# The second layer's MLP as seven block products: float32 block sums on GpSimd, split into halves before each product

## The chip, the cores and the metric

One Trainium2 chip, of which one core is used. The metric is the device time of one execution in microseconds; lower is better. Engines are named as in the profile: PE (TensorE, matmuls), PEld (its weight loads), DVE (VectorE), ACT (ScalarE), POOL (GpSimd), SP (SyncE, which here only issues DMAs).

## The reference

A backbone of two layers over 1024 latent tokens and 256 context tokens, width 1024, all in float32. Layer 0 mixes with two kinds of attention, layer 1 with a state-space scan and a gated unit (GLU); each layer ends in an MLP with a hidden width of 4096:

```python
def _mlp(h, w1, w2):
    return jnp.square(jax.nn.relu(h @ w1)) @ w2
...
        h2 = _rmsnorm(x, norm2_g[i], NORM_EPS) * (1.0 + sc2) + sh2
        x = x + g2 * _mlp(h2, mlp_w1[i], mlp_w2[i])
...
    return _rmsnorm(x, final_g, NORM_EPS)
```

In layer 1 only the 1024 latent tokens go on, so its MLP is two matrix products, 1024 x 1024 by 1024 x 4096 and back.

## The kernel before

The residual stream `xl` stays on chip, feature by token; `xv1(ct, b)` (line 1083) is feature tile `ct` (128 of 1024) of the half `b` (512 tokens). Float32 operands are multiplied as three products of halves: a value is rounded to the matmul's own 32-bit format (`hi`, on ACT) and the rest is subtracted out (`lo`, on DVE), and `mm3` (line 312) issues hi·hi, hi·lo and lo·hi for each pair of tiles, each a 128x128 weight against 128x512 tokens.

`mlp` (line 1124) runs over 16 slices `f` of the hidden width, 256 columns each. For each it loads two 512 KB pages of W1 and two of W2 (`weights`, line 301, which also splits them), multiplies the normed input halves `Hh[b]` and `Hl[b]` (eight feature tiles) by W1, takes Relu and Square on ACT, the same square and the remainder on DVE (lines 1140 to 1143), multiplies by W2 and adds each result tile to the stream with one DVE instruction (`add_x`, line 1091), a multiply by the gate and an add, straight from the accumulator. For layer 1 nothing else runs beside it.

Before it stands `glu` (line 1580), which goes through half 0 and then half 1. After each half, `follow` and `rstd_steps` (lines 391 and 322) collect squares, sum them on PE (`n_st`, `n_tk`), take a reciprocal root and spread it (`n_bc`), and `scaled` (line 435) writes the normed input: a DVE multiply, a POOL scale and shift, then the split into `Hh` and `Hl` (`to_H`, line 1093). Half 0's norm runs beside half 1's GLU; half 1's runs while the MLP has only half 0 to work on. After the last slice the same steps serve the final norm (`final`, line 1608), whose results are stored on SP.

The order of instructions is chosen by a scheduler that takes what is ready, by priority, except in stages that use `Plan` (line 112). There each step carries an engine, a fixed cost, a rank (its due time), what it comes after and which buffers it takes and gives; `order` (line 142) lists the steps by the time at which they could start by those costs plus 0.05 of their rank, and every engine's queue is laid down in that order. A queue is worked off strictly in order. Before the change the attention and the scan (`ssm`, line 1408) use it. Memory comes from pools stacked from the left and the right; a tile laid on memory of an earlier pool waits for the last user of what it covers.

## Time and profile before

| | us |
|---|---|
| three runs before | 3135.32, 3137.86, 3138.17 |
| median of them | 3137.86 |
| the profiled execution | 3133.75 |
| its span, first to last instruction | 3132.0 |
| in it: layer 1's MLP, from the GLU's last matmul to its own last | 2402.8 to 3114.1 |
| in it: final norm and stores after that | 3114.1 to 3132.0 |

The mean granted clock of the span is 0.98. All positions in the text are microseconds from the span's start in the profiled execution.

### The profile page before, as it was taken

How to read it: one execution, taken by the hardware profiler on the slowest of the kernel's cores; microseconds unless marked ns; L12 is line 12 of the kernel's file. 1: busy time of each engine (PE TensorE's matmuls, PEld its weight loads, DVE VectorE, ACT ScalarE, POOL GpSimd, SP SyncE). 2: the span in 40 equal slices, each digit the busy share in tenths (PEclk: the TensorE clock that was granted, in tenths of full speed). 3: DMA queues.
4: the chain of work that ended last, by engine and by line, in shares of the span. 5: the costliest groups of instructions: out<-in, count | busy, mean ns of one | idle time of the engine just before them, and what ended most of it. 6: DMA issues, size and time to landing. Idle time of an engine off the chain costs nothing.

```text
span 3132.0 us, 46329 instructions
## 1 busy us (share of the span) xinstructions
PE 2949.1 (94%) x17736; PEld 2435.7 (78%) x17736; DVE 1844.6 (59%) x3225; ACT 969.1 (31%) x1843; POOL 1128.4 (36%) x2314
## 2 busy tenths in 40 slices
PE   7999998889999999999999999777899999999998
PEld 4878887777778778777888888566787888888886
DVE  4887677997653655455454454699524554455444
ACT  3322125766652311111211211445323212212122
POOL 3352224555432577777884000477323000000001
PEclk9999999999999999999999999888999999999999
DMA  6356564324533234334111101566212111111111
GB/s 237 108 199 228 199 216 132 88 71 118 158 94 123 88 106 122 107 121 92 60 59 54 41 30 37 174 184 179 85 61 88 53 42 54 41 54 53 42 54 54
DMA packets 171149, 321.53 MB, mean 103 GB/s; under 512 B 34560, under 2 KB 97056, under 8 KB 170928
## 3 DMA queue, kind: packets, MB, share of 16 engines
q1 hardware_dynamic: 165840, 302.24, 30.9%
q0 software_dynamic: 5088, 16.34, 1.6%
...
## 4 chain that ended last, share of the span: by engine, by line
PE 77%; DVE 13%; issue 3%; DMA 3%; ACT 2%; POOL 2%; SPq 0%; DVEq 0%; POOLq 0%; ACTq 0%
PE m_acc L317 17%; PE m_acc L318 16%; PE m_acc L319 16%; DVE s_ab L1506 2%; PE at_bank L740 2%; PE at_sc L732 2%; PE g_acc L319 2%; PE g_acc L317 2%; PE g_acc L318 2%; PE ip_acc L317 2%; PE ada_acc L269 2%; PE ip_acc L318 2%; PE ip_acc L319 2%; PE at_bank L1023 2%; DVE s_ab L1494 1%
## 5 line engine op out<-in xcount | busy, mean ns | idle before, releaser
L1091 DVE SCALAR_TENSOR_TENSOR xl<-m_acc,m,xl 128x512 f32<-128x512 f32 x512 | 378.7, 748 | 222.0 <-PE m_acc L319 221.7
L317 PE MATMUL m_acc<-hid_h,w_hi 128*128 128x512 f32 (+1 forms) x1280 | 476.8, 372 | 0.0
L317 PE MATMUL m_acc<-Hh,w_hi 128*128 128x512 f32 (+1 forms) x1280 | 473.4, 370 | 0.9 <-ACT Hh L453 0.9
L318 PE MATMUL m_acc<-hid_l,w_hi 128*128 128x512 f32 (+1 forms) x1280 | 472.4, 369 | 0.0
L318 PE MATMUL m_acc<-Hl,w_hi 128*128 128x512 f32 (+1 forms) x1280 | 471.8, 369 | 0.5 <-DVE Hl L454 0.5
L319 PE MATMUL m_acc<-hid_h,w_lo 128*128 128x512 f32 (+1 forms) x1280 | 471.8, 369 | 0.0
L319 PE MATMUL m_acc<-Hh,w_lo 128*128 128x512 f32 (+1 forms) x1280 | 471.4, 368 | 0.0
L308 ACT ACTIVATE w_hi<-w_raw 128x1024 fp32r<-128x1024 f32 x196 | 202.5, 1053 | 796.1 <-PE m_acc L318 688.8
L309 DVE TENSOR_TENSOR w_lo<-w_raw,w_hi 128x1024 fp32r<-128x1024 f32 x196 | 244.3, 1261 | 214.3 <-ACT w_hi L308 204.9
L1142 DVE TENSOR_TENSOR m_r<-m_r 128x512 f32<-128x512 f32 (+1 forms) x160 | 103.9, 651 | 407.8 <-ACT hid_h L1141 407.6
L425 POOL TENSOR_TENSOR rs_y<-n_v,mhalf 128x4 f32<-128x4 f32 (+1 forms) x13 | 12.4, 950 | 763.3 <-DVE n_v L373 763.3
L317 PEld LDWEIGHTS m_acc<-hid_h,w_hi 128*128 128x128 f32 x1280 | 241.2, 188 | 56.7 <-issue 15.2
L317 PEld LDWEIGHTS m_acc<-Hh,w_hi 128*128 128x128 f32 x1280 | 241.4, 189 | 47.1 <-issue 5.8
L318 PEld LDWEIGHTS m_acc<-hid_l,w_hi 128*128 128x128 f32 x1280 | 241.3, 189 | 44.3 <-issue 5.0
L318 PEld LDWEIGHTS m_acc<-Hl,w_hi 128*128 128x128 f32 x1280 | 241.5, 189 | 40.9 <-DVE Hl L454 2.1
L319 PEld LDWEIGHTS m_acc<-hid_h,w_lo 128*128 128x128 f32 x1280 | 241.3, 189 | 40.4
L319 PEld LDWEIGHTS m_acc<-Hh,w_lo 128*128 128x128 f32 x1280 | 241.4, 189 | 40.0
L1140 ACT ACTIVATE m_r<-m_acc 128x512 f32<-128x512 f32 (+1 forms) x160 | 87.9, 551 | 440.4 <-PE m_acc L319 436.4
L317 PE MATMUL ip_acc<-Hh,w_hi 128*128 128x512 f32 (+1 forms) x384 | 141.6, 370 | 4.1 <-ACT Hh L453 4.1
L318 PE MATMUL ip_acc<-Hl,w_hi 128*128 128x512 f32 (+1 forms) x384 | 138.1, 360 | 1.4 <-DVE Hl L454 1.2
L319 PE MATMUL ip_acc<-Hh,w_lo 128*128 128x512 f32 (+1 forms) x384 | 137.5, 359 | 0.0
L732 PE MATMUL at_sc<-at_k,at_q 128*128 128x256 f32 (+2 forms) x608 | 125.1, 336 | 10.9 <-ACT at_p L822 4.3
...
## 6 DMA issues: line engine op xcount, KB each, us to landing
w_raw<-in_w_dram SPq DMA_DIRECT2D x128, 512.0 KB, 4.1
...
```

What stands on the lines that cost most here:

```text
L269: nc.tensor.matmul(acc[32 * q:32 * q + 32, 256 * half:256 * half + 256], self.act[:, 4 * kg + q, :], r[:, q, :], start=(kg == 0), stop=(kg ...
L308: nc.scalar.activation(hi[:, j], r, AF.Copy)
L309: nc.vector.tensor_tensor(lo[:, j], r, hi[:, j].bitcast(F32), ALU.subtract)
L317: nc.tensor.matmul(out, lh, rh, start=first and i == 0, stop=False)
L318: nc.tensor.matmul(out, lh, rl, start=False, stop=False)
L319: nc.tensor.matmul(out, ll, rh, start=False, stop=last and i == n - 1)
L732: PE.matmul(sc[:, c:c + n], qd["q"][:, m, hl, qo:qo + P], k["k"][m][:, k0:k0 + n], start=(hl == 0), stop=(hl == 1))
L740: PE.transpose(tp[:kw, P * j:P * j + P], p[:, c0 + P * j:c0 + P * j + kw], self.ident)
L1023: PE.matmul(grp["pv"][64 * hh:64 * hh + 64, u, :], hd["v"][:kw, vt, 64 * hh:64 * hh + 64], st["aT", (hh, i)][:kw, P * (j % 4):P * (j % 4) ...
L1091: nc.vector.scalar_tensor_tensor(xv, av, gate, xv, op0=ALU.mult, op1=ALU.add)
L1140: nc.scalar.activation(r[:, :n], acc[:, :n], AF.Relu)
L1142: nc.vector.tensor_tensor(r[:, :n], r[:, :n], r[:, :n], ALU.mult)
```

## The change

Layer 1's MLP is done by Strassen's scheme in Winograd's form. Each of four slices `f` of 1024 hidden columns has two units, one for W1 and one for W2, and a unit is a product of two 1024x1024 matrices cut into 2 x 2 blocks of 512: seven block products in place of eight, with weight sums s1 to s4 and token sums t1 to t4 of 512x512 blocks, and sums of the results. The host lays the weights out as 1 MB blocks (`w1b`, `w2b`); those of layer 0 keep their pages.

A product is four steps (one for each tile of 128 along the inner width); a step is 12 matmuls, three for each of four accumulator banks. Before each step a weight tile and a token tile, 128x512 each, are split by one ACT and one DVE instruction into one of four slots per operand. The sums run on POOL, float32, 32 of 128x512 per unit. In W1 units the token blocks are the normed input in float32 (`Hr`); the token sums go to r1, r2, r3. In W2 units they are the hidden blocks and most sums are made in place. Products that share terms accumulate on the banks of an earlier one after it has been copied out (`ON`). Product 1 of a W2 unit, which goes to three blocks of the stream, is copied out scaled by ACT into the four r2 tiles, and 12 POOL instructions add it to the stream; the other six are added by DVE as before. The order of products is 1, 6, 2, 7, 5, 4, 3, in the first unit 1, 2, 6, 7, 5, 4, 3. All of it is laid out by a `Plan`.

The GLU's `scaled` now writes `Hr` on POOL, without the split. `Hr` (two halves of 16 KB per partition) takes the memory under the GLU's weight pages; the new weight blocks and split slots take that of `Hh` and `Hl`, the other new tiles that of the pages. The final norm's tiles are views of tiles that are then free.

```diff
+    a["w1b"] = g["mlp_w1"][1].reshape(2, 4, P, 4, 2, 512).transpose(3, 4, 0, 2, 1, 5).reshape(4, 2, 2, P, 2048)
+    a["w2b"] = g["mlp_w2"][1].reshape(4, 2, 4, P, 2, 512).transpose(0, 4, 1, 3, 2, 5).reshape(4, 2, 2, P, 2048)
...
+            o = to(ct) if to else t[:, :n]
+            nc.gpsimd.tensor_scalar(o, t[:, :n], G[:, ct, m:m + 1], self.mv(i, part, ct, m), op0=ALU.mult, op1=ALU.add)
+            if put:
+                put(ct, o)
...
+    ON = {2: 1, 7: 6, 4: 7, 3: 5}
+
+    def mlp_s(self, mp, wp, ps):
...
+        for q in "ab":
+            blocks += [wp.tile([P, 4, 512], F32, name=f"st_w{q}{j}") for j in range(2)]
+            slots[q] = [wp.tile([P, 2, 512], F32R, name=f"st_{q}{j}") for j in range(4)]
...
+        r2 = [mp.tile([P, 512], F32, name=f"st_r2{t}") for t in range(4)]
...
+        plan = Plan(rings, lead=10.0)
...
+        for u in range(8):
+            f, second, last = u // 2, u % 2, u == 7
+            order = (1, 2, 6, 7, 5, 4, 3) if u == 0 else (1, 6, 2, 7, 5, 4, 3)
...
+            for (m, k), p in (((0, 0), 1), ((1, 0), 6), ((1, 1), 6), ((0, 1), 2)):
+                ld[m, k] = plan.add("D", 5.6, at[p] - 30, F(load, m, k), take=["A"], issue=0.7)
...
+                    if p == 6:
+                        made["s1", t] = plan.add("G", 1.4, r - 14, lambda t=t, A=A: vt(s1[:, t], A[1, 0][:, t], A[1, 1][:, t], ALU.add),
...
+                    if second:
+                        gh = lambda k, n: [(f"h{k}{n}{t}", hm["take", k, n, t])]
+                        if p == 6:
+                            made["t1", t] = plan.add("G", 1.4, r - 13, F(vt, r1[t], b12, b11, ALU.subtract), [hd(0, 1), hd(0, 0)], take=[f"r1{t}"])
+                            made["t3", t] = plan.add("G", 1.4, r - 12.5, F(vt, b12, b22, b12, ALU.subtract), [hd(1, 1), made["t1", t]])
+                            made["t2", t] = plan.add("G", 1.4, r - 12, F(vt, b11, b22, r1[t], ALU.subtract), [made["t1", t], made["t3", t], *sp[1, t, "b"]])
...
+                    def hi(w, t=t, sl=sl, av=av, bv=bv, A=A, tm=tm):
+                        sl[w] = T(w, slots[w]), av(A, t) if w == "a" else tm["r3", t] if bv is None else bv
+                        S.activation(sl[w][0][:, 0], sl[w][1], AF.Copy)
+
+                    def lo(w, sl=sl):
+                        V.tensor_tensor(sl[w][0][:, 1], sl[w][1], sl[w][0][:, 0].bitcast(F32), ALU.subtract)
...
+                        hs[w] = plan.add("S", 0.56, r - 8, F(hi, w), after, take=[w])
+                        ls[w] = plan.add("V", 0.66, r - 7.5, F(lo, w), [hs[w]], give=give)
...
+                        for mt in range(4):
+                            c = slice(P * mt, P * mt + P)
+                            for i, (x, y) in enumerate(((l[:, 0, c], h[:, 0]), (l[:, 0, c], h[:, 1]), (l[:, 1, c], h[:, 0]))):
+                                PE.matmul(bk[p][mt], x, y, start=(p not in self.ON and t == 0 and i == 0), stop=(t == 3 and i == 2), skip_group_check=True)
...
+                        if p == 3:
+                            x = plan.add("V", 0.72, rk, F(ev, c12, c12, 3), [pe, made["u2", t]], give=giveX(5))
+                            relu2(c12, c12, rk + 0.5, [x], (0, 1, t))
+                    else:
+                        if p == 1:
+                            for m, g in ((0, g1), (1, g2)):
+
+                                o = r2[(2 * t + m) % 4]
+                                c = plan.add("S", 0.58, rk + 0.1 * m, lambda o=o, g=g, ps_=ps_: S.activation(o, ps_(1), AF.Copy, scale=g), [pe], take=[f"r2{(2 * t + m) % 4}"])
+                                outs.append(c)
+                                for x in ((x12,) if m == 0 else (x21, x22)):
+                                    made.setdefault("xu", []).append(plan.add("G", 1.4, rk + 2 + m, F(vt, x, x, o, ALU.add), [c], give=[(f"r2{(2 * t + m) % 4}", c)]))
...
-            self.scaled(lambda ct: self.xv1(ct, b), 512, 1, 1, 0, bc, sp, self.to_H(b))
+            self.scaled(lambda ct: self.xv1(ct, b), 512, 1, 1, 0, bc, sp, to=lambda ct: self.Hr[b][:, ct])
...
+            rp = es.enter_context(net.pool("hr"))
+            net.Hr = [rp.tile([P, KT, 512], F32, name=f"hr{b}") for b in range(2)]
...
-                with net.pool("mlp1") as mp:
-                    net.mlp(1, (0, 1), net.xv1, ps, mp, lambda: None, lambda: net.follow(net.xv1, ps, mp, lambda b, bc: net.final(b, bc, mp)))
+            hs.close()
+            with net.pool("mlp1") as mp, net.pool("mlp1w", side="right") as wp, net.pool("ps5", space=PSUM) as ps:
+                net.mlp_s(mp, wp, ps)
```

## Rows read from the trace of the kernel before

**Rows 1.** The page, part 1: busy time, share of the span and instructions.
```profile
PE 2949.1 (94%) x17736; PEld 2435.7 (78%) x17736; DVE 1844.6 (59%) x3225; ACT 969.1 (31%) x1843; POOL 1128.4 (36%) x2314
```
**Rows 2.** Windows: stretch, us, busy PE PEld DVE ACT POOL, clock, DMA share, GB/s.
```profile
2402.80:2428.10 25.30, 21.50 (x98) 14.91 (x96) 13.67 (x23) 8.79 (x14) 10.85 (x10) 1.00 0.13 42
...
2441.00:3093.00 652.00, 652.00 (x2878) 540.11 (x2877) 322.26 (x418) 131.08 (x182) 0.00 (x0) 1.00 0.15 47
...
3114.10:3132.00 17.90, 5.09 (x25) 3.72 (x24) 6.75 (x13) 1.40 (x3) 1.70 (x2) 0.59 0.43 165
...
2200.00:2222.00 22.00, 13.24 (x65) 11.00 (x63) 16.36 (x26) 7.52 (x14) 10.88 (x13) 0.84 0.08 28
```
**Rows 3.** Groups by line, 2402.8 to 3132: count | busy us, mean ns | idle before.
```profile
L317 PE MATMUL m_acc<-hid_h,w_hi 128*128 128x512 f32 x512 | 199.5, 390 | 0.0
...
L1091 DVE SCALAR_TENSOR_TENSOR xl<-m_acc,m,xl 128x512 f32<-128x512 f32 x256 | 189.2, 748 | 104.7 <-PE m_acc L319 104.7
...
L1143 DVE TENSOR_TENSOR hid_l<-m_r,hid_h 128x512 fp32r<-128x512 f32 x64 | 44.0, 689 | 1.6
L1141 ACT ACTIVATE hid_h<-m_r 128x512 fp32r<-128x512 f32 x64 | 40.1, 629 | 1.5
L1140 ACT ACTIVATE m_r<-m_acc 128x512 f32<-128x512 f32 x64 | 37.8, 593 | 185.9 <-PE m_acc L319 184.4 <-DVE hid_l L1143 1.5
```
**Rows 4.** Windows of the MLP's accumulators alone, the first stretch.
```profile
2402.80:2428.10 25.30, 18.94 (x73) 12.90 (x72) 0.00 (x0) 0.14 (x1) 1.00 0.13 42
```
**Rows 5.** Timeline of DVE, operations in a row: start, us.
```profile
2430.78 1.29 DVE L1143 TENSOR_TENSOR hid_l<-m_r,hid_h 128x512 fp32r<-128x512 f32 x2
...
3123.44 5.36 DVE L1618 SCALAR_TENSOR_TENSOR f_o<-xl,vecs,n_bc 128x512 f32<-128x512 f32 x8 [2.17 <-PE n_bc L382]
```
**Rows 6.** Timeline of POOL in the GLU.
```profile
2239.06 1.29 POOL L1604 TENSOR_TENSOR xl<-xl,g_sg 128x512 f32<-128x512 f32 x1 [24.48 <-DVE g_sg L1602]
2249.16 2.20 POOL L1604 TENSOR_TENSOR xl<-xl,g_sg 128x512 f32<-128x512 f32 x1 [8.81 <-DVE g_sg L1602]
2252.10 1.29 POOL L356 TENSOR_TENSOR n_sq<-n_sq 128x512 f32<-128x512 f32 x1 [0.74 <-ACT n_sq L351]
```
**Rows 7.** Timeline of DVE in the GLU, the operations beside those.
```profile
2239.17 2.26 DVE L309 TENSOR_TENSOR w_lo<-w_raw,w_hi 128x1024 fp32r<-128x1024 f32 x1 [0.19 <-ACT w_hi L308]
...
2249.00 1.22 DVE L309 TENSOR_TENSOR w_lo<-w_raw,w_hi 128x1024 fp32r<-128x1024 f32 x1
```
**Rows 8.** Timeline of POOL in the final norm.
```profile
3106.83 2.55 POOL L1620 TENSOR_TENSOR f_o<-xl,f_r 128x512 f32<-128x512 f32 x2 [2.51 <-ACT f_r L1613]
```
**Rows 9.** Timeline of DVE beside them (`m_acc` is an accumulator).
```profile
3107.55 0.75 DVE L1091 SCALAR_TENSOR_TENSOR xl<-m_acc,m,xl 128x512 f32<-128x512 f32 x1
```
**Rows 10.** The chain that ended last, between GLU and MLP: start, us, what.
```profile
2408.72 1.07 PE n_st L336 x8
...
2410.91 0.80 PE n_tk L371 x8
...
2413.64 1.17 PE n_bc L382 x8
...
2427.42 0.64 ACT Hh L453
```
**Rows 11.** Timeline of POOL: the scalings of half 1.
```profile
2415.63 2.82 POOL L448 TENSOR_SCALAR n_t<-n_t,G,m 128x512 f32<-128x512 f32 x3 [2.63 <-DVE n_t L447]
```
**Rows 12.** Timeline of PE: the scan's last readout, the GLU's first matmul.
```profile
2217.92 0.61 PE L1532 MATMUL s_y<-s_T,s_U 128*128 128x128 f32 x4
...
2221.91 0.50 PE L317 MATMUL g_acc<-Hh,w_hi 128*128 128x512 f32 x1 [1.82 <-ACT w_hi L308]
```
**Rows 13.** Timeline of SP: issues of the GLU's pages.
```profile
2197.42 0.33 SPq L307 DMA_DIRECT2D w_raw<-in_glua_dram  x1
...
2223.14 0.33 SPq L307 DMA_DIRECT2D w_raw<-in_glua_dram  x1
```
**Rows 14.** Timeline of ACT: the first use of such a page.
```profile
2226.85 1.06 ACT L308 ACTIVATE w_hi<-w_raw 128x1024 fp32r<-128x1024 f32 x1 [4.04 <-DMA w_raw<-in_glua_dram]
```

More of the change, by code (lines that the diff above doesn't have):

```diff
@@ L54, in host_layout @@
     a["glub"] = pages(g["glu_w_b"][0])
-    a["w1"] = np.stack([pages(g["mlp_w1"][i]) for i in range(2)])
-    a["w2"] = g["mlp_w2"].reshape(2, 32, P, D)
+    a["w1"] = pages(g["mlp_w1"][0])
+    a["w2"] = g["mlp_w2"][0].reshape(32, P, D)
+    a["w1b"] = g["mlp_w1"][1].reshape(2, 4, P, 4, 2, 512).transpose(3, 4, 0, 2, 1, 5).reshape(4, 2, 2, P, 2048)
+    a["w2b"] = g["mlp_w2"][1].reshape(4, 2, 4, P, 2, 512).transpose(0, 4, 1, 3, 2, 5).reshape(4, 2, 2, P, 2048)
     rpb = g["na_rpb"][0]
@@ L196, in run, with __init__, tile @@
                 s["fn"]()
+class Views:
+    def __init__(self, pool, **views):
+        self.pool, self.views, self.turn = pool, views, dict.fromkeys(views, 0)
+    def tile(self, shape, dt, name=None, tag=None, bufs=None):
+        if tag not in self.views:
+            return self.pool.tile(shape, dt, name=name, tag=tag, bufs=bufs)
+        self.turn[tag] += 1
+        return self.views[tag][(self.turn[tag] - 1) % len(self.views[tag])]
 class Net:
@@ L433, in newton, with scaled @@
         V.scalar_tensor_tensor(r, t, 1.5, y, op0=ALU.add, op1=ALU.mult)
-    def scaled(self, xv, n, i, which, m, bc, sp, put):
+    def scaled(self, xv, n, i, which, m, bc, sp, put=None, to=None):
         nc = self.nc
@@ L447, in scaled @@
             nc.vector.tensor_tensor(tv, xx, bv, ALU.mult)
-            nc.gpsimd.tensor_scalar(t[:, :n], t[:, :n], G[:, ct, m:m + 1], self.mv(i, part, ct, m), op0=ALU.mult, op1=ALU.add)
-            put(ct, t[:, :n])
+            o = to(ct) if to else t[:, :n]
+            nc.gpsimd.tensor_scalar(o, t[:, :n], G[:, ct, m:m + 1], self.mv(i, part, ct, m), op0=ALU.mult, op1=ALU.add)
+            if put:
+                put(ct, o)
     def split(self, hi, lo, src):
@@ L1127, in mlp @@
         for f in range(16):
-            w1 = self.weights(a["w1"][i, 2 * f:2 * f + 2])
-            w2 = self.weights(a["w2"][i, 2 * f:2 * f + 2])
+            w1 = self.weights(a["w1"][2 * f:2 * f + 2])
+            w2 = self.weights(a["w2"][2 * f:2 * f + 2])
             hid = {}
@@ L1701, in build @@
                     return
-        with net.pool("H1", side="right") as hp:
-            H(hp, range(2))
+        with ExitStack() as hs:
+            H(hs.enter_context(net.pool("H1", side="right")), range(2))
             with net.pool("ssm") as sp, net.pool("ps3", space=PSUM) as ps:
@@ L1711, in build @@
                     net.glu(ps, sp)
-                if stop("glu"):
-                    return
-                with net.pool("mlp1") as mp:
-                    net.mlp(1, (0, 1), net.xv1, ps, mp, lambda: None, lambda: net.follow(net.xv1, ps, mp, lambda b, bc: net.final(b, bc, mp)))
+            if stop("glu"):
+                return
+            hs.close()
+            with net.pool("mlp1") as mp, net.pool("mlp1w", side="right") as wp, net.pool("ps5", space=PSUM) as ps:
+                net.mlp_s(mp, wp, ps)
 def kernel(**inputs):
```

171 lines of the change are left out of this document (added).

## The prediction

> **What bounds the kernel now.** I read the page's busy line first: PE is busy 94% of the span [rows 1]. As that is an average over stages, the windows come next, cut where the second layer's MLP begins and ends [rows 2]. From 2441 to 3093 us PE is busy 652.00 of 652.00 us at a granted clock of 1.00; DVE is busy 322, ACT 131, POOL 0. The stage is bound by the number of matmuls: 652.00 us / 2877 = 0.2266 us each. (The 390 ns "mean of one" in the groups overlaps its neighbours [rows 3]; only the spacing counts.) The six groups of 512 give 3072 matmuls. Ahead of it the MLP's own matmuls number 73 in 25.30 us [rows 4], 16.5 us of work, so 8.8 us are lost to the norm of the second half of the tokens. Behind it come 17.9 us of final norm and stores. All stands against the profiled execution, 3133.75 us, 4.1 below the median 3137.86; I add the 4.1 at the end.
>
> **The change, part by part.**
>
> *Matmuls.* Each of the 8 units (W1 or W2 of one f) falls from 8 products of 48 matmuls to 7: 3072 becomes 2688. 384 x 0.2266 = **-87.0 us**. The spacing should hold: W2 changed bank every 6 matmuls inside the window without a gap, now it is every 3, with the same shapes. A unit then takes 336 x 0.2266 = 76.1 us, a pair (W1, W2) 152.3.
>
> *Splits.* Per product and step one weight and one token operand are cut: 56 pairs (ACT hi, DVE lo) per unit. ACT's lasts 0.63 us, DVE's 0.69 [rows 3]; two DVE ones in a row take 1.29 us, so one costs 0.60 [rows 5]. The old weight splits and the two DVE operations per hidden tile go. DVE per pair: 112 x 0.60 + 44 evictions x 0.66 (eight in 5.36 us [rows 5]) = 96.2 of 152.3 us. ACT: 112 splits and 44 copies, Relus and Squares, 156 x 0.63 = 98 us. Neither bounds by itself; if they did, PE would wait in the middle of products.
>
> *Sums on POOL.* New work: 32 sums of 128x512 in a W1 unit, 44 in a W2 unit (12 add product 1 to x), 76 per pair. A sum alone takes 1.29 us, but 2.20 when a DVE subtraction of two SBUF operands began 0.16 us before it [rows 6, 7]: it ended 1.14 us after that subtraction did. The other way round, a subtraction that began 0.11 us after a POOL sum took 2.26 instead of 1.22 [rows 6, 7]. So each holds the other up to its end. DVE operations with one operand in PSUM don't: two POOL operations of a sum's kind, 2.55 us together, lie beside such ones, the one shown of 0.75 us [rows 8, 9]. Only splits collide with sums: per pair 67.2 + 76 x 1.14 = 153.8 us of a thing that one of the two can have at a time, against 152.3 us of PE. That is even, so nothing is left to make up a delay, and order decides. [...] The Trainium skill (Perfetto Trace Analysis, section "Optimizing Scalar/DVE Operations") warns that moving work between the two might not help; its strong reading is rival C.
>
> *From W1 to W2 (four times).* Say product 3, W1's last, ends at E. Product 6 of W2 needs hidden block (0,1), which product 3 completes: eviction, Relu and Square (0.75 + 0.59 + 0.63 [rows 3], the first bank being done 2 us before E), then on POOL t1, t3, t2 for four tiles, 12 sums. At 1.29 each they end at E+15.8; with 6 splits and four s2 sums between, at E+24.6. Hi and lo add 1.3. Product 6's last step, due at E+19.1, is late by 0 to 6.8. Product 1's eviction then takes eight copies through four r2 tiles; the later four wait for six x sums queued behind the t sums, 7.7 to 11.3 us and a copy of 0.6, so E+24 to E+36.5, where product 2's third bank is due at E+23.2; behind those copies in ACT's queue stand the hi splits of the next steps. The two share a queue, so the second delay holds the first: 1 to 13 us. Two splits come with each 2.72 us step, so I take 10, near the contended end: **+40 us** in all (4 to 52). The other crossing, W2 to W1, needs only Hr, which is there: nothing, covered by some 20 us of POOL time before product 6.
>
> *Start.* Before: 8.8 us lost. After: the split slots lie where Hh[1] and Hl[1] were, so the first split waits for the GLU's last matmul: hi and lo, about 1.5 us. The norm's small matmuls on PE stay, 3.0 us (1.07, 0.80, 1.17 [rows 10]). Products 1 and 2 need Hr[0] alone, 21.8 us of cover. Product 6 needs sums over Hr[1]. POOL's eight scalings begin at 2415.63, three in 2.82 us [rows 11], so end near 2423; behind them come, as the planner's ready times order them, 8 t sums, two t3 and 12 s sums: 22 x 1.29 = 28.4 us, up to 8.4 more for 14 splits, 1.3 for the last split. Product 6's last step can begin between 2452.8 and 2461.2; unhindered it would at 2437.3. So 20 to 28 us are lost, or 5 if the s sums go first while POOL is idle; I take 23, **+14.2 us** net. The Hh/Hl splits that leave the norm's chain (its last links are such, 2427.42 [rows 10]) count in this.
>
> *GLU's start.* The new hr pool takes 32 KB under the page buffers, which now lie on the scan's T and U tiles, one of them read until the last readout matmul at about 2218.5 [rows 12]. The first page, issued at 2197.42 before, must wait till then, with the second behind it on SP; one that was issued at 2223.14 was in use at 2226.85 [rows 13, 14]. PE's first GLU matmul goes from 2221.91 to about 2223.4: **+2 us** (0 to 5).
>
> *Costed at nothing.* Loads: 1 MB blocks, four per 76 us, against 128 pages of half that size now at 0.15 of the DMA [rows 2]; the first are hidden by the GLU, whose first half frees their space; nothing else stands on SP until the stores. End: four banks complete in the last step and are added in one pass, as the last tile was; the norm's chain is unchanged: 0 (-1 to +4).
>
> Sum: -87.0 + 14.2 + 40 + 2 = **-30.8 us**; profile 3103, median **3107 us**.
>
> **Rivals.**
> A is this sum.
> B: sums and splits slide past each other. Crossings cost 3, the start 8: -87 - 0.8 + 12 + 2 = -74, **3064**. For it: 153.8 against 152.3 is no excess, PE has four slots per operand to run ahead, and evictions leave POOL free. Against it: the x sums stand behind t sums whatever the lock does.
> C, the other side: DVE becomes the bound. Every POOL sum stops the split queue for its full 1.14 us: 96.2 + 86.6 = 182.8 us per pair, 30.5 over PE, +122 in place of +40: **3189**. The place is DVE's queue, where evictions stand behind a stopped split. It decides from (152.3 + 17.7 - 96.2) / 76 = 0.97 us per sum, 17.7 being a pair's share of the other terms' gain. For it: POOL has 64% of a pair's time in bare work, and the planner that orders the queues knows nothing of the collision (1.4 and 0.66 are fixed costs there). Against it: in [rows 8] sums run freely beside evictions, and 44 of those lie in a pair.
> D: seven products don't cost seven eighths. If a bank change every three matmuls cost 11.5 ns each, 2688 of them eat the 31 us: no change, **3138**. Against it: no gap within [rows 2].
> E: PE's waits at crossings let the clock fall to the lower of its two levels. It stood at 0.84 and 0.59 where PE idled much [rows 2], at 1.00 with 21.5 of 25.3 us busy [rows 2]. 96 matmuls at half pace per W2 unit are 21.8 us, +87 in all: **3194**. PE should not idle that long in one piece.
>
> **How the numbers follow.** A 0.52, B 0.20, C 0.18, D 0.06, E 0.04. About 0.2%, 6.3 us, is what a measurement of this kernel can tell from no change. Faster: A and B, 0.72; same: D, 0.06; slower: C and E, 0.22. The time is A's, 3107. The range goes from a little under B, 3058 (low ends of the start and the crossings), to 3172, which takes in A's own upper end (52 at the crossings, 28 at the start: 3124) and C at two thirds of its price; the rest of C and E, under 0.2, stays out. The own range of A and B together is 3058 to 3124.
>
> **What would show it.** Matmuls in the MLP: 2688 at 0.2266 us. POOL busy some 390 us there, its sums mostly over 1.29 us, and many DVE splits over 0.69. PE's idle time should sit in products 6 and 2 of W2 units, released by splits of POOL's t sums and by copies through r2, some 10 us per unit, with W1 units near 76 us and one long wait before the first product 6. I am wrong if PE waits spread evenly over all steps (C), if W2 units take 76 to 80 us (B), if matmuls are spaced wider without waits (D), or if the granted clock falls inside the MLP (E).

## The result, and the profile after

The changed kernel takes **3187.91 us** (median of four runs, 3183.45 to 3194.56) against 3136.59 before (four runs): a ratio of **1.0166, 95% interval 1.0146 to 1.0185**. It is slower by 51 us where I forecast 31 less, and above my range's upper end, 3172. Its profiled execution is the one of 3183.45 us, with a span of 3181.4 (before: 3132.0), so 49.4 us have to be found.

The page, part 1, answers to [rows 1]:

```profile
PE 2913.2 (92%) x17352; PEld 2388.0 (75%) x17352; DVE 2091.5 (66%) x3385; ACT 1169.3 (37%) x2259; POOL 1602.4 (50%) x2618
```

384 matmuls are gone; DVE is busy 247 us more and POOL 474. Next the windows (columns as in [rows 2]), cut at the GLU's last matmul, at the first matmul of units 0 to 3 and of unit 7, and at the last matmul of unit 7. Even units are W1, odd ones W2.

```profile
2402.40:2413.80 11.40, 5.13 (x25) 3.65 (x25) 2.60 (x7) 5.97 (x11) 2.28 (x2) 0.68 0.00 0
2413.80:2515.20 101.40, 84.44 (x339) 67.10 (x339) 72.46 (x86) 44.89 (x83) 57.84 (x40) 0.92 0.12 42
2515.20:2623.80 108.60, 88.09 (x338) 67.61 (x337) 83.48 (x79) 41.83 (x73) 90.79 (x61) 0.89 0.11 39
2623.80:2700.00 76.20, 76.20 (x338) 63.17 (x337) 64.15 (x75) 46.20 (x85) 34.82 (x23) 1.00 0.16 56
2700.00:2801.10 101.10, 85.45 (x337) 66.05 (x336) 90.24 (x83) 41.38 (x72) 85.10 (x55) 0.92 0.12 42
...
3054.80:3153.00 98.20, 85.86 (x356) 65.62 (x354) 74.90 (x77) 43.89 (x77) 59.52 (x38) 0.93 0.00 1
3153.00:3181.40 28.40, 9.72 (x47) 5.59 (x46) 13.45 (x24) 4.42 (x8) 9.78 (x10) 0.58 0.38 148
```

Unit 2 is what the change promised: 336 matmuls in 76.20 us, PE never idle, clock 1.00, although POOL does 23 operations in it beside the splits; units 4 and 6 are the same. The W2 units take 98 to 109 us. In unit 3 DVE is busy 90.24 us where PE's own work is 76.2; in unit 7, behind which no unit follows, it is busy 74.90. PE's busy time grows too (85.45 in place of 76.20 in unit 3), at a granted clock of 0.92: PE idles, and runs part of what follows at the lower level.

The terms of my sum against these windows, before's own from [rows 2]:

| term | forecast | measured | from |
|---|---|---|---|
| matmuls | -87.0 | -87.0 | 384 x 0.2266; units 2, 4, 6 at 76.20 |
| from W1 to W2 | +40 | **+104.4** | 108.6 + 101.1 + 101.3 + 98.2 less 4 x 76.2 |
| start | +14.2 | **+27.8** | gap 11.4, unit 0 over by 25.2, less the 8.8 lost before |
| GLU's start | +2 | -0.4 | the GLU ends at 2402.4, before at 2402.8; its first matmul alone is 1.6 later against the scan's end (see below) |
| end | 0 | **+10.5** | 28.4, before 17.9 |
| losses at the old MLP's end | not in the sum | -6.4 | 2402.8 to 3114.1 less 696.1 of matmuls, less 8.8 |

They add up to 48.9 of the 49.4 us.

GLU's start, in the changed kernel: the first page is issued when the scan's last readout ends (2217.3), and PE's first GLU matmul follows 5.0 us after that end (4.9 to 5.3 in all twelve traces with the change), where it was 3.4 before. The total hides it, because in this execution the readout ended 1.3 us earlier and the GLU itself took 0.9 less.

```profile
2217.29 0.33 SPq L323 DMA_DIRECT2D w_raw<-in_glua_dram  x1
...
2222.27 0.79 PE L333 MATMUL g_acc<-Hh,w_hi 128*128 128x512 f32 x1 [3.44 <-ACT w_hi L324]
```

Where in a unit? I counted 48 matmuls per product and took the time from a product's first matmul to the next one's (unhindered: 10.9 us). In order 1, 6, 2, 7, 5, 4, 3 unit 3 takes 11.9, **26.0**, 13.7, 11.3, **16.6**, 10.9, 10.9. Unit 5 is the same to 0.1; unit 1 has 33.5 in product 6.

Groups of the MLP (columns as in [rows 3]; L1312 is the DVE split, L1238 the POOL sum) and PE's waits from 2402.4 to 3153 (us in total, times, longest):

```profile
L1326 PE MATMUL st_b<-st_b,st_a 128*128 128x512 f32 x2688 | 656.2, 405 | 81.1 <-ACT st_b L1309 33.5 <-DVE st_b L1312 29.5 <-ACT st_r L1388 8.8
...
L1312 DVE TENSOR_TENSOR st_a<-st_wa,st_a 128x512 fp32r<-128x512 f32 x100 | 121.4, 1216 | 51.9 <-ACT st_a L1309 51.7
...
L1238 POOL TENSOR_TENSOR xl<-xl,st_r 128x512 f32<-128x512 f32 x48 | 77.6, 1653 | 0.0
L1357 DVE SCALAR_TENSOR_TENSOR xl<-st_b,m,xl 128x512 f32<-128x512 f32 x96 | 65.3, 738 | 0.0
```

```profile
PE st_b L1326 <- ACT st_b L1309: 33.5, 13, 5.4
PE st_b L1326 <- DVE st_b L1312: 29.5, 20, 2.9
PE st_b L1326 <- ACT st_r L1388: 8.8, 8, 1.5
PE st_b L1326 <- DVE st_h L1354: 6.1, 1, 6.1
```

PE waits for splits (L1309, L1312) of token operands and for the copies of product 1 (L1388). A split averages 1.05 to 1.26 us in the larger groups, where two in a row cost 1.29 together before [rows 5]; a sum on `xl` 1.65. The adds from a bank (L1357) stay at 0.74: they collide with nothing.

The seam into unit 3, that is, the stretch where a W1 unit hands over to a W2 unit (W1 ends at E = 2700.0). POOL's timeline, DVE's, ACT's and PE's, then the windows of its first 38 us and of what follows:

```profile
2685.30 1.76 POOL L1238 TENSOR_TENSOR st_s<-st_wa,st_wb 128x512 f32<-128x512 f32 x1 [28.09 <-DMA st_wb<-in_w2b_dram]
...
2697.32 1.68 POOL L1238 TENSOR_TENSOR st_wa<-st_s,st_wa 128x512 f32<-128x512 f32 x1 [3.89 <-DVE st_a L1312]
...
2706.01 1.69 POOL L1238 TENSOR_TENSOR st_r<-st_h,st_h 128x512 f32<-128x512 f32 x1 [1.30 <-ACT st_h L1345]
...
2720.30 1.28 POOL L1238 TENSOR_TENSOR st_s<-st_wa,st_wb 128x512 f32<-128x512 f32 x1
...
2727.51 1.70 POOL L1238 TENSOR_TENSOR st_h<-st_h,st_r 128x512 f32<-128x512 f32 x1
2729.17 19.41 POOL L1238 TENSOR_TENSOR xl<-xl,st_r 128x512 f32<-128x512 f32 x12
2748.54 5.15 POOL L1238 TENSOR_TENSOR st_h<-st_h,st_h 128x512 f32<-128x512 f32 x3
```

```profile
2701.78 1.78 DVE L1312 TENSOR_TENSOR st_b<-st_h,st_b 128x512 fp32r<-128x512 f32 x1
2703.48 2.47 DVE L1354 TENSOR_TENSOR st_h<-st_h,st_b 128x512 f32<-128x512 f32 x4
...
2726.34 5.09 DVE L1312 TENSOR_TENSOR st_a<-st_wb,st_a 128x512 fp32r<-128x512 f32 x3
2731.36 6.79 DVE L1312 TENSOR_TENSOR st_b<-st_h,st_b 128x512 fp32r<-128x512 f32 x4
```

```profile
2704.19 1.23 ACT L1344 ACTIVATE st_h<-st_h 128x512 f32<-128x512 f32 x2 [3.12 <-DVE st_h L1354]
```

```profile
2729.92 0.80 PE L1326 MATMUL st_b<-st_b,st_a 128*128 128x512 f32 x1 [4.94 <-ACT st_b L1309]
2733.16 6.21 PE L1326 MATMUL st_b<-st_b,st_a 128*128 128x512 f32 x17 [2.44 <-DVE st_b L1312]
```

```profile
2700.00:2738.00 38.00, 27.99 (x98) 20.50 (x97) 28.88 (x23) 17.13 (x31) 36.15 (x24) 0.82 0.00 0
2738.00:2764.00 26.00, 23.31 (x99) 18.01 (x99) 26.00 (x22) 11.56 (x20) 25.37 (x17) 1.00 0.06 20
```

Product 3's evictions (L1354) begin at E+3.5, behind two splits that sums had stopped to 1.78 us each; the Relu (L1344) waits 3.12 us for them, and the first t sum 1.30 us for the Square (L1345). So the t sums begin at E+6.0, and the last one ends at E+29.2, in a row of 15 sums at 1.55 us each: twelve t sums and, from 2720.30, three s sums that stood behind nine of them. Product 6's last step follows at 2733.16 = E+33.2. Then the twelve x sums go on for 19.4 us and t4 behind them, and from 2726.3 to 2738.2 DVE does no more than seven splits: **one split and one sum take 1.70 us together, so a step of two splits takes 3.40, where PE needs 2.72**. In the first 38 us the row on POOL decides, which is busy 36.15 of them; DVE, busy for 28.88, waits for it by way of ACT's hi splits. Behind that, to 2764, DVE is busy without a gap.

Unit 1 begins otherwise. Its first t sum stood at the head of POOL's queue for 42.90 us, with all twelve s sums behind it, so that 24 sums come after W1's end:

```profile
2517.93 1.29 POOL L1238 TENSOR_TENSOR st_r<-st_h,st_h 128x512 f32<-128x512 f32 x1 [42.90 <-ACT st_h L1345]
```

The start, in time: ScalarE's first hi split (L1309) stands behind the norm's n_e, the first lo split behind its Newton steps (the n_r row is the last); on PE the norm's last small matmuls (L398) stand ahead of the first product and wait for n_r too.

```profile
2407.63 0.60 ACT L382 ACTIVATE n_e<-n_st 128x512 f32<-128x512 f32 x1 [1.68 <-PE n_st L352]
2408.12 0.62 ACT L1309 ACTIVATE st_a<-st_wa 128x512 fp32r<-128x512 f32 x1
...
2411.87 0.16 DVE L449 SCALAR_TENSOR_TENSOR n_r<-rs_t,rs_y 128x4 f32<-128x4 f32 x1
2411.95 0.69 DVE L1312 TENSOR_TENSOR st_a<-st_wa,st_a 128x512 fp32r<-128x512 f32 x1
...
2412.09 2.07 PE L398 MATMUL n_bc<-ident,n_r 128*128 128x128 f32 x8 [1.94 <-DVE n_r L449]
2413.81 4.60 PE L1326 MATMUL st_b<-st_b,st_a 128*128 128x512 f32 x13
```

The tail: the last product's four tiles come due together at 3153.0; their adds (L1357) wait behind the first scaling of half 0 (L1879), and the sums of squares (L352) take 1.93 us at a granted clock of 0.58.

```profile
3157.51 0.75 DVE L1879 SCALAR_TENSOR_TENSOR hr<-xl,vecs,st_b 128x512 f32<-128x512 f32 x1 [1.88 <-ACT st_h L1874]
...
3158.18 2.06 DVE L1357 SCALAR_TENSOR_TENSOR xl<-st_b,m,xl 128x512 f32<-128x512 f32 x3
...
3162.83 1.93 PE L352 MATMUL st_b<-st_r,ones 128*32 128x512 f32 x8 [2.33 <-ACT st_r L367]
```

### The profile page after: what moved, and what is told of

It reads as the page before. It is cut to its first block, busy times and chain, and to the rows that moved or that the text cites. A ratio compares the mean times of both kernels' runs of the same rounds, so it can differ in the third digit from the quotient of the medians.

```text
span 3181.4 us, 46889 instructions
## 1 busy us (share of the span) xinstructions
PE 2913.2 (92%) x17352; PEld 2388.0 (75%) x17352; DVE 2091.5 (66%) x3385; ACT 1169.3 (37%) x2259; POOL 1602.4 (50%) x2618
## 4 chain that ended last, share of the span: by engine, by line
PE 67%; DVE 16%; POOL 8%; issue 4%; ACT 3%; DMA 2%; SPq 0%; DVEq 0%; POOLq 0%; ACTq 0%
PE st_b L1326 13%; PE m_acc L333 10%; PE m_acc L334 9%; PE m_acc L335 9%; PE at_bank L758 2%; DVE s_ab L1767 2%; PE at_sc L750 2%; PE g_acc L333 2%; PE g_acc L335 2%; PE g_acc L334 2%; DVE st_b L1312 2%; PE at_bank L1041 2%; PE ip_acc L333 2%; POOL st_h L1238 2%; PE ada_acc L285 2%
## 5 line engine op out<-in xcount | busy, mean ns | idle before, releaser
L1326 PE MATMUL st_b<-st_b,st_a 128*128 128x512 f32 x2688 | 656.2, 405 | 81.1 <-ACT st_b L1309 33.5
L1326 PEld LDWEIGHTS st_b<-st_b,st_a 128*128 128x128 f32 x2688 | 521.4, 196 | 216.4 <-ACT st_b L1309 45.8
L333 PE MATMUL m_acc<-hid_h,w_hi 128*128 128x512 f32 (+1 forms) x768 | 277.5, 361 | 0.0
L333 PE MATMUL m_acc<-Hh,w_hi 128*128 128x512 f32 (+1 forms) x768 | 273.9, 357 | 0.0
L334 PE MATMUL m_acc<-hid_l,w_hi 128*128 128x512 f32 (+1 forms) x768 | 273.1, 356 | 0.0
L335 PE MATMUL m_acc<-hid_h,w_lo 128*128 128x512 f32 (+1 forms) x768 | 272.5, 355 | 0.0
L334 PE MATMUL m_acc<-Hl,w_hi 128*128 128x512 f32 (+1 forms) x768 | 272.3, 354 | 0.0
L335 PE MATMUL m_acc<-Hh,w_lo 128*128 128x512 f32 (+1 forms) x768 | 272.2, 354 | 0.0
L1109 DVE SCALAR_TENSOR_TENSOR xl<-m_acc,m,xl 128x512 f32<-128x512 f32 x256 | 189.7, 748 | 117.6 <-PE m_acc L335 117.1
L334 PEld LDWEIGHTS m_acc<-Hl,w_hi 128*128 128x128 f32 x768 | 145.4, 189 | 19.2
L1312 DVE TENSOR_TENSOR st_a<-st_wa,st_a 128x512 fp32r<-128x512 f32 x100 | 121.4, 1216 | 51.9 <-ACT st_a L1309 51.7
```

Source lines behind the costliest of these rows:

```text
L333: nc.tensor.matmul(out, lh, rh, start=first and i == 0, stop=False)
L334: nc.tensor.matmul(out, lh, rl, start=False, stop=False)
L335: nc.tensor.matmul(out, ll, rh, start=False, stop=last and i == n - 1)
L1109: nc.vector.scalar_tensor_tensor(xv, av, gate, xv, op0=ALU.mult, op1=ALU.add)
L1312: V.tensor_tensor(sl[w][0][:, 1], sl[w][1], sl[w][0][:, 0].bitcast(F32), ALU.subtract)
L1326: PE.matmul(bk[p][mt], x, y, start=(p not in self.ON and t == 0 and i == 0), stop=(t == 3 and i == 2), skip_group_check=True)
```

## The experiments

The theories: **T** (T2 once the first four runs gave it prices), the time is lost at the seams, where POOL's sums stand in a row beside splits; **C**, my rival, collisions cost evenly; **O**, the order and bare amounts of POOL's work alone; **L**, late weight blocks; **Q** (in e6), DVE's work in the unit, wherever the sums stand. Unit lengths in us, measured as above; the tail is what follows the last matmul of unit 7. In these executions the GLU ended between 2402.4 and 2413.4, by the same instructions, so units are a safer measure than totals:

| kernel | median us | 0 | 1 | 2 | 3 | 4 | 5 | 6 | 7 | tail |
|---|---|---|---|---|---|---|---|---|---|---|
| changed | 3187.9 | 101.3 | 108.6 | 76.2 | 101.2 | 76.2 | 101.3 | 76.2 | 98.2 | 28.4 |
| e1_no_lo | 3115.5 (one) | 83.2 | 97.2 | 76.2 | 84.7 | 76.2 | 84.5 | 76.2 | 87.0 | 28.4 |
| e2_s_first | 3187.0 | 102.2 | 107.4 | 76.5 | 98.6 | 76.5 | 100.0 | 76.2 | 98.3 | 28.4 |
| e6_s_ahead | 3181.0 | 100.2 | 103.1 | 76.4 | 97.7 | 76.8 | 97.6 | 76.4 | 97.5 | 28.4 |
| e3_t_dve | 3151.5 | 100.2 | 96.9 | 76.2 | 91.8 | 76.2 | 91.8 | 76.2 | 92.6 | 28.4 |
| e4_x_direct | 3160.6 | 100.6 | 99.2 | 76.2 | 93.1 | 76.2 | 92.8 | 76.2 | 95.6 | 28.4 |
| f1_all_dve | 3117.1 | 88.8 | 86.6 | 76.4 | 86.0 | 76.4 | 85.3 | 76.4 | 88.7 | 29.5 |
| g2_chain_pool | 3160.0 | 101.4 | 93.5 | 76.2 | 93.9 | 76.2 | 94.8 | 76.2 | 96.1 | 28.4 |
| g1_chain | 3093.7 | 89.3 | 82.4 | 76.2 | 80.2 | 76.3 | 80.2 | 76.3 | 82.8 | 29.4 |
| g3_chain_tail | 3096.4 | 89.3 | 82.4 | 76.2 | 80.2 | 76.2 | 80.2 | 76.3 | 81.6 | 31.4 |
| h2_w1_dve | 3160.4 | 88.1 | 103.0 | 76.2 | 95.6 | 76.2 | 94.5 | 76.2 | 98.2 | 28.4 |
| h1_tiles | 3091.5 | 88.1 | 82.4 | 76.2 | 80.2 | 76.2 | 80.2 | 76.2 | 89.9 | 18.4 |

**e1_no_lo: the lo splits left out, the sums kept.** The matmuls read the hi halves in their place, so their number stays.

```diff
-hs[w] = plan.add("S", 0.56, r - 8, F(hi, w), after, take=[w])
-ls[w] = plan.add("V", 0.66, r - 7.5, F(lo, w), [hs[w]], give=give)
+hs[w] = ls[w] = plan.add("S", 0.56, r - 8, F(hi, w), after, take=[w], give=give)
```

> This kernel leaves out every lo split on VectorE (L1312) and lets the matmuls read the hi halves three times, so the number of matmuls, sums and weight-side activations stays and only 448 VectorE subtractions go. Theory T (the time is lost in the seams between a unit of W1 and one of W2, where POOL's chain of sums for product 6 runs beside splits and each slows the other): sums fall from a mean of 1.58 us to 1.28 to 1.4; units 3, 5 and 7 fall from about 101 us to 85 to 88; unit 1 stays at 100 or more, because there the sums were late by their place in the queue; units 2, 4, 6 stay at 76.2; total 35 to 55 us less. Theory C (VectorE's queue is the bound throughout): every unit falls to about 76, total some 100 us less. Theory O (POOL's bare work and its order alone, no contention): no change beyond 10 us.

3115.49 us, one run: 72 us less than the changed kernel's median, more than T's 35 to 55. Units 3, 5 and 7 lie within 0.5 us of T's 85 to 88; unit 1 came down to 97.2, where T had 100 or more, and unit 0 by 18, which T had not counted. With no splits on DVE every sum is bare:

```profile
L1238 POOL TENSOR_TENSOR xl<-xl,st_r 128x512 f32<-128x512 f32 x48 | 59.5, 1280 | 0.0
```

Product 6 of unit 3 falls from 26.0 to 12.5. So O's "no change beyond 10 us" is out, and C's 76 us in every unit as well. A part is left to bare amounts: product 2 of unit 3 rises from 13.7 to 17.8, and 8.5 of the unit's 25 us stay. In unit 1, 21 of 32 us are left: 24 sums in a row are long even bare. The run takes DVE's split work away with the collisions and can't tell the two apart; f1 does.

**e2_s_first: the s sums ahead in POOL's queue.** Only the ranks of s1, s3 and s2 change, by 30, and with them the planner's lead for loads:

```diff
-made["s1", t] = plan.add("G", 1.4, r - 14, ...
+made["s1", t] = plan.add("G", 1.4, r - 44, ...
-plan = Plan(rings, lead=10.0)
+plan = Plan(rings, lead=30.0)
```

> Same instructions; on POOL the twelve sums of blocks of weights (s1, s3, s2) of a unit of W2 stand ahead of the sums of hidden blocks in the queue, in units 3, 5 and 7 only the last three are moved (they stood behind nine t sums), in unit 1 all twelve. Theory T with the order deciding: product 6 falls in unit 1 from 33.5 us to 20 to 24, in units 3, 5, 7 from 26 to 20 to 23; unit 0 within 5 us of before, as its 24 sums are the same in number; total 20 to 30 us less. Theory C: no change of the total beyond 8 us, since VectorE has the same work. Theory L (the blocks of W2 land too late): product 6 stays at 26 in units 3, 5, 7.

No gain: ratio to before 1.0162 (1.0142 to 1.0182), where T had 20 to 30 us and C at most 8. Product 6 fell further than T had it, to 17.6 in units 1, 3, 5 and 7, so L in that form is out; but product 1 rose (unit 3: 11.9 to 15.2; unit 1: 11.7 to 24.1) and so did product 2 (13.7 to 19.2). The order within POOL's row decided which product waits, not how long they wait together. My reading, not shown by this run alone: what PE needs is the row's end. In unit 1 the edit did less than its expectation says: two t sums still stood ahead of the twelve s sums, and POOL waited there as before. That called for e6.

**e6_s_ahead: the s sums ahead for certain.** The s sums of all four steps are planned first, and t1 gets a dependency:

```diff
-made["t1", t] = plan.add("G", 1.4, r - 13, F(vt, ...), [hd(0, 1), hd(0, 0)], ...)
+made["t1", t] = plan.add("G", 1.4, r - 13, F(vt, ...), [hd(0, 1), hd(0, 0), made["s2", 3]], ...)
```

> In each unit of W2 the first t sum on POOL waits until all twelve s sums are done (a dependency in the plan, nothing else), so that in unit 1 they stand ahead of it in the queue; with the ranks alone two t sums stayed ahead of them there. In unit 1 POOL then has idle time from some 2500 us on, where it waited 42.90 us for a hidden block, to do most of the s sums before W1 ends. Theory T2 (what PE waits for is the end of POOL's row): unit 1 loses 10 to 12 sums of 1.3 to 1.6 us from the row behind its start and falls from 108.6 us to 88 to 95; units 3, 5, 7, whose blocks land only 15 us before their start, stay within 4 us of 101, 101 and 98; total 10 to 20 us less than the changed kernel. Theory Q (it is only the vector engine's work in the unit that counts, whatever the place of the sums): unit 1 stays above 103.

Ratio 1.0127 (1.0099 to 1.0155), 7 us less, an interval that overlaps the changed kernel's. Unit 1 went to 103.1: T2's 88 to 95 failed, its 10 to 20 us of the total too, and Q's bound (above 103) is met by a hair only. Units 3, 5 and 7 stayed within T2's 4 us. POOL's first rows of the unit, which begins at 2523.4, say why:

```profile
2519.89 6.65 POOL L1238 TENSOR_TENSOR st_s<-st_wa,st_wb 128x512 f32<-128x512 f32 x4 [35.47 <-DMA st_wa<-in_w2b_dram]
2526.50 5.97 POOL L1238 TENSOR_TENSOR st_wa<-st_wa,st_wa 128x512 f32<-128x512 f32 x4
```

The sums were free to run, but their last block landed 3.5 us before the unit. There are four buffers, and the last products of the unit before still read the one it goes into. So L holds in another form than I gave it: late blocks don't delay product 6 by themselves, they keep the s sums from being done ahead, in unit 1 and, by the 28.09 us on the same kind of load, in unit 3. A fifth buffer was not tried.

**e3_t_dve: the t sums of W2 on DVE.**

```diff
-made["t1", t] = plan.add("G", 1.4, r - 13, F(vt, r1[t], b12, b11, ALU.subtract), ...
+made["t1", t] = plan.add("V", 0.62, r - 13, F(vt, r1[t], b12, b11, ALU.subtract, V), ...
```

> The sixteen sums of hidden blocks (t1, t3, t2, t4) of each unit of W2 go from POOL to VectorE, where such a sum should take 0.6 to 0.7 us and a POOL sum 1.3 to 1.7. Theory T: product 6 loses most of its excess (26 us to 11 to 16 in units 3, 5, 7; unit 1 from 33.5 to under 20), total 45 to 60 us less. Theory C: VectorE gets 16 x 0.65 = 10 us more per unit of W2 and saves the contention of 16 sums, total within 15 us of the changed kernel or slower. Theory L: product 6 stays above 20.

Ratio 1.0043 (1.0027 to 1.0060), 36 us less than the changed kernel: between the theories (T 45 to 60, C within 15). Product 6 of unit 3 went to 12.9, so the blocks' landing alone doesn't set it (the s sums still waited for the same load), but products 1 and 2 rose to 17.0 and 17.2, with splits behind t sums and copies behind x sums. The first x sum of unit 3 shows something new; first POOL, then DVE beside it:

```profile
2704.61 6.48 POOL L1238 TENSOR_TENSOR xl<-xl,st_r 128x512 f32<-128x512 f32 x1 [4.85 <-ACT st_r L1388]
```

```profile
2705.04 0.68 DVE L1238 TENSOR_TENSOR st_h<-st_h,st_r 128x512 f32<-128x512 f32 x1
...
2709.25 0.69 DVE L1312 TENSOR_TENSOR st_b<-st_h,st_b 128x512 fp32r<-128x512 f32 x1
```

Eight DVE operations that began after the sum went ahead of it, at their bare 0.60 each; it was done 1.15 us after the last had ended (2711.09 against 2709.94).

**e4_x_direct: product 1 added to x from its bank.** Twelve adds on DVE for eight copies and twelve x sums:

```diff
-c = plan.add("S", 0.58, rk + 0.1 * m, lambda o=o, g=g, ps_=ps_: S.activation(o, ps_(1), AF.Copy, scale=g), [pe], ...)
-    made.setdefault("xu", []).append(plan.add("G", 1.4, rk + 2 + m, F(vt, x, x, o, ALU.add), [c], ...))
+for x, g in ((x12, g1), (x21, g2), (x22, g2)):
+    outs.append(plan.add("V", 0.75, rk, F(xa, x, g, 1), [pe]))
```

> Product 1 of a unit of W2 is added to the residual by VectorE straight from its bank: twelve scalar_tensor_tensor of about 0.75 us take the place of eight copies on ScalarE, the ring of r2 buffers and twelve sums on POOL. Theory T: the waits behind the x sums go, product 2 by 2.8 us and product 5 by 5.7 us in units 1, 3 and 5, and product 2 in unit 7; product 6 stays at 26; total 20 to 30 us less. Theory C: VectorE gets 12 x 0.75 = 9 us more per unit, which at most balances the twelve collisions it loses: total within 10 us of the changed kernel.

Ratio 1.0077 (1.0059 to 1.0096), 27 us less, as T said and C did not: in unit 3 product 2 fell to 11.4 and product 5 to 10.9, and product 6 stayed at 26.3. Twelve operations were added to DVE, and it came off better (in unit 3 busy 85.79 us in place of 90.24): the adds from a bank don't collide, and the twelve collisions of the x sums are gone. The eight copies on ACT went with them, so the waits for those are part of the gain.

**f1_all_dve: every sum on DVE.** All thirteen `plan.add("G", 1.4, ...` of sums become `plan.add("V", 0.62, ...`, and `vt` runs on VectorE.

> Every sum of blocks (L1238, 76 per pair of units) goes from POOL to VectorE; POOL has no work in the MLP. Theory T2 (formed on the first four runs: from the end of a unit of W1 POOL has some 19 sums to do before product 6's last step, then 12 x sums, at 1.6 to 1.7 us each beside splits; and such a sum delays VectorE by some 1.1 us, where VectorE would do it itself in 0.6): a unit of W2 then asks VectorE for 56 splits, 44 sums and 24 residual adds at a pitch of 0.60 to 0.66 us, 76 us in all, so units 3, 5, 7 fall from 101 us to 78 to 88, unit 1 from 109 to under 92, unit 0 from 101 to 83 to 92; units 2, 4, 6 stay at 76; total 80 to 110 us less than the changed kernel (3078 to 3108). Theory O (only order and bare amounts count, so a longer vector queue puts the splits later): units 3, 5, 7 stay above 92 as with the t sums alone moved, total within 25 us of that run's 3151.

Ratio **0.9934** (0.9917 to 0.9950), 71 us less: units 0, 1, 3, 5 as T2 said, unit 7 just over, the total 9 us above its range. The same 304 sums cost DVE 0.69 us each, and splits are back at theirs:

```profile
L1312 DVE TENSOR_TENSOR st_b<-st_h,st_b 128x512 fp32r<-128x512 f32 x96 | 66.1, 688 | 0.0
...
L1238 DVE TENSOR_TENSOR xl<-xl,st_r 128x512 f32<-128x512 f32 x48 | 29.4, 690 | 1.3 <-ACT st_r L1388 1.3
```

It does all the work of the changed kernel and gains what leaving out the lo splits did (e1). So the loss comes from doing the two kinds of work beside each other on two engines, and not from DVE having splits to do. How much of the 71 us is the collisions and how much the shorter sum (0.69 us on DVE, 1.28 bare on POOL) this run does not part.

**h2_w1_dve: only W1's sums on DVE.** The same edit, with `gq = ("G", 1.4) if second else ("V", 0.62)`.

> The changed kernel with the sums of the units of W1 alone (32 per unit, L1238) on VectorE; those of the units of W2 stay on POOL. Theory T2 (sums spread over a unit are hidden, the time goes where POOL's sums stand in a row at the seam into W2): units 2, 4, 6 stay at 76.2 us although half of all collisions are gone from them, units 3, 5, 7 stay within 4 us of 101, 101 and 98; unit 0, whose 32 sums stand in a row behind the normalization, falls from 101 to 87 to 91; total 8 to 22 us less than the changed kernel. Theory C (collisions cost evenly, wherever they are): 128 of 304 collisions gone, so some 40 us less, spread over units 0, 2, 4 and 6.

Ratio 1.0073 (1.0056 to 1.0090), 28 us less, above T2's 22. Units 2, 4 and 6 don't move, unit 0 hits, and the gain isn't C's even spread. T2's miss is units 3 and 5, 6 to 7 us shorter where I allowed 4: product 5 fell from 16.6 to 10.9. The row had gone on with the next W1 unit's sums beside product 5's splits, and these now left it.

**g2_chain_pool and g1_chain: another order and other banks in W2.** Product 1's bank takes products 6, 7 and 4 on top, product 2 has its own bank, then 5 and 3; 28 adds in place of 24 and the copies and x sums gone. The weight blocks' loads follow the new order. g2 leaves the sums on POOL, g1 puts them on DVE.

```diff
-order = (1, 2, 6, 7, 5, 4, 3) if u == 0 else (1, 6, 2, 7, 5, 4, 3)
+order = (1, 2, 6, 7, 5, 4, 3) if u == 0 or second else (1, 6, 2, 7, 5, 4, 3)
+on, same = ({6: 1, 7: 6, 4: 7, 3: 5}, {5: 2}) if second else (self.ON, {})
...
 if p == 1:
+    outs.append(plan.add("V", 0.75, rk, F(xa, x11, g1, 1), [pe]))
```

> Sums stay on POOL. In a unit of W2 the products run in the order 1, 2, 6, 7, 5, 4, 3 on two sets of banks: product 1's bank is added to the residual once (four adds by VectorE) and then takes products 6, 7 and 4 on top of it, product 2 has the other set, which then holds 5 and 3. The twelve x sums, the eight ScalarE copies and the wait of product 2 for them go; residual adds on VectorE are 28 in place of 24; product 7 has to wait for the four adds of product 6. Theory T2: product 6 has 10.9 us more cover, its excess falls from 15 us to 0 to 6, waits behind x sums vanish, product 7 gains 2 to 4; units 3, 5, 7 at 80 to 90; total 45 to 75 us less than the changed kernel. Theory C (VectorE's queue): its work hardly changes (4 adds more, 12 collisions fewer per unit), total within 15 us.

> Both: all sums on VectorE, and the order and banks of the run before this one in the units of W2. VectorE then has 56 splits, 32 sums and 28 adds per unit of W2, some 71 us of 76. Theory T2: units 1, 3, 5, 7 at 77 to 82 (product 7's wait for four adds, 2 to 4 us, stays), unit 0 at 83 to 92, total 95 to 125 us less than the changed kernel (3063 to 3093). Theory O: units of W2 above 88, total above 3115.

g2: ratio 1.0066 (1.0049 to 1.0083), 28 us less; T2's 45 to 75 was too much. One product's cover more doesn't help where every step takes 3.40 us: its unit 3 (in order 1, 2, 6, 7) has 10.9, 15.1, 22.1, 13.2, with DVE and POOL in lockstep. First DVE, then POOL:

```profile
2706.30 1.78 DVE L1313 TENSOR_TENSOR st_a<-st_wb,st_a 128x512 fp32r<-128x512 f32 x1
2708.00 1.77 DVE L1313 TENSOR_TENSOR st_b<-st_h,st_b 128x512 fp32r<-128x512 f32 x1
```

```profile
2707.61 1.62 POOL L1239 TENSOR_TENSOR st_h<-st_h,st_h 128x512 f32<-128x512 f32 x1
2709.19 1.74 POOL L1239 TENSOR_TENSOR st_h<-st_h,st_r 128x512 f32<-128x512 f32 x1
```

g1: ratio **0.9856** (0.9842 to 0.9871), 46 us under the kernel before and 66 under g2, which differs only in who does the sums. Units 3 and 5 are as T2 said; units 1 and 7 and the total lie up to 0.8 us above its ranges. Its window of unit 3 and PE's waits in it:

```profile
2662.70:2742.80 80.10, 76.95 (x337) 62.80 (x336) 74.49 (x120) 36.41 (x64) 0.00 (x0) 1.00 0.15 53
```

```profile
PE st_b L1327 <- DVE xl L1358: 1.6, 1, 1.6
PE st_b L1327 <- DVE st_b L1313: 1.6, 2, 1.1
```

DVE in unit 3: 90.24 us changed, 74.49 here. Of the 4 us that are left, 1.6 are product 7's wait for product 6's adds, as expected, and 1.6 waits for splits in product 6.

**g3_chain_tail and h1_tiles: the tail.** g3 issues half 0's last norm step after product 3's adds; h1 instead runs the last product output tile by output tile:

```diff
+for i in range(4):
+    for k in range(4):
+        lastpe = plan.add("PE", PK / 4, at[p] + PK * (i + k / 4), F(part, i, k), [*tm[p][k][1:], lastpe, *made["free", 5]])
```

> As the run before, and the last step of half 0's final norm is issued after the four residual adds of product 3, so that these stand ahead of half 0's scalings in VectorE's queue. Reading of the tail (the adds waited 5 us there behind the first scaling): the tail from the last matmul of product 3 to the end falls by 3 to 6 us, and nothing else moves. Rival: half 0's own scalings, now 3 us later, push back half 1's Newton steps on POOL and VectorE, so that the tail falls by less than 2 us or grows.

> The kernel with all sums on VectorE and the new order and banks, and in the last product (3 of unit 7) the matmuls run output tile by output tile in place of block of K by block of K, so that three of its four tiles can be added and squared before the last is done. Reading of the tail (28.4 us after the last matmul, against 17.9 before, because four tiles come due at once): product 3 waits 1 to 3 us for its fourth pair of splits at its start, the tail falls from 29.4 us to 22 to 25, total 3 to 6 us less than the same kernel without it (3088 to 3091). Rival (the tail is the two norms' chains at the low clock, whatever the tiles): the tail stays at 28 us or more and the total is the same or 1 to 3 us more.

g3: ratio 0.9866 (0.9852 to 0.9881), the tail 31.4 in place of 29.4: the rival was right, half 0's chain only moved behind the adds. h1: ratio **0.9852** (0.9837 to 0.9866), 3091.49 us, 2.2 under g1's median and not to be told from it. In the trace unit 7 and the tail together take 108.4 us, against 82.8 + 29.4 = 112.2, within the 3 to 6 us expected, but neither part is as expected: the tail falls to 18.4 (22 to 25 expected), and product 3 takes 20.6 in place of 13.5 (a wait of 1 to 3 expected), with more of half 0's norm matmuls inside it. It has the lowest median here, 47 us under the kernel before.

## Why the prediction was wrong

**Matmuls**: right to 0.1 us a unit (76.20 in units 2, 4 and 6, where I had 76.1). Bank changes cost nothing, so D was wrong.

**The step that failed: the crossing from W1 to W2, +40 us (10 a unit), which measured 104.4 (25 in units 3 and 5).** Its first part, "product 6's last step late by 0 to 6.8", was 14.1 (E+33.2 where E+19.1 was due). I had costed eviction, Relu and Square as three bare operations and left out the queues before them: my sum has the t sums begin at about E+0.3, and they began at E+6.0, because the evictions stood behind stopped splits. The row itself, 15 sums in 23.2 us, was no longer than the contended 24.3 that I had allowed. After it the last hi and lo took 4.0 us, not 1.3: three splits of weights stood before the lo, each beside a sum. In unit 1 product 6 lost 22.6 us, as all twelve s sums, where I had four s2, stood behind its first t sum. The second delay, which I took as held by the first, was 2.8 us in product 2 on top, and product 5 lost 5.7 more, which I had nowhere: the x sums didn't free POOL, and behind them the next W1 unit's sums went on (h2), all beside splits at 3.40 us per step.

**Under it lies an average.** I set 153.8 us of splits and sums against 152.3 of PE per pair of units and took it for even. DVE is busy 64.15 + 90.24 = 154.4 us over a pair, stops included (another sum than mine, which left out the evictions). But it is 64 in the W1 unit, whose PE time hides it, and 90 in the W2 unit, 14 over PE. Splits run at most four steps ahead, so the 12 us to spare in the one never reach the other. Even a unit is too wide a stretch: in unit 7 DVE is busy 74.90 us, less than PE needs, and products 1, 6 and 2 take 11.9, 26.1 and 13.6 all the same, by the row on POOL.

**C's number, 3189, came true by luck, its mechanism only in part.** The crossings cost 104.4 us and not C's 122; the start and the end, which C had as A did, made up for it. Its price is right: in a row, each sum stops the split queue for 1.10 us. Of its place, "evictions stand behind a stopped split" is what happened at E, and from 2738 to 2764 DVE is the bound; but from 2700 to 2738, where most is lost, DVE idles for 9 us, and W1 units 2, 4 and 6 show no wait at all. By my own sum 1.14 was already beyond the 0.97 us from which C decides; my argument against it, that sums run freely beside evictions, says nothing of the price beside splits. Asked of the W2 unit alone, the same sum gives (152.3 / 2 + 8.9 - 33.6 - 24 x 0.66) / 44 = 0.81 us per sum (8.9 is half of 17.7).

**A's place was right in the main, its size was not**: 15.1 and 2.8 of unit 3's 25 us went into products 6 and 2, by splits of t sums and by copies, as I said it would if A held; product 5's 5.7 did not. **B** is refuted by the rows in which split and sum alternate. Rival **E**: the clock does fall in the seams, to 0.82 from 2700 to 2738 and 0.92 over unit 3, and PE's busy time in the unit grows by 9.2 us, where I had 21.8 for E. With the waits gone (g1) it is 1.00. What the lower clock adds to the waits, and what of it lies hidden in them, no run parts.

**Start**: the gap ahead of the first matmul was 11.4 us, where I had 4.5 (1.5 for the first split, 3.0 for the norm's matmuls). I had costed the operations and not the queues: the first lo came 9.6 us after the GLU's end (2402.4 to 2411.95), behind the norm's own steps, and on PE the norm's last matmuls stood ahead of the first product and waited for the same steps. Which of the two sets the gap was not tested in any run; it stays open what moving the split ahead is worth. Unit 0's sums came, as I ordered them, t first; they collided more than the 8.4 us I allowed: e1, without collisions, gives back 18 of its 25 us, and f1, with the sums on DVE, 12.5.

**GLU's start** was forecast rightly: PE's first matmul came 1.6 us later against the readout, and the -0.4 of the table is the stages around it. **End** was 10.5, not 0: I saw that four banks come due at once and costed only the last tile's add. Four adds, four squares and their sums on a PE at 0.58 follow in turn. Changing the order of the adds (g3) did not help; the tiles' coming earlier (h1) shortened unit 7 and the tail by 3.8 us in the trace, which the medians don't confirm.

On moving work between these two engines the Trainium skill (Perfetto Trace Analysis, section "Optimizing Scalar/DVE Operations") warns that it might not help, as they share a port. The runs say more: beside a busy DVE a POOL sum takes 1.10 us from DVE, which does it itself at 0.60.
